# Where the operands of the second FFN products lie in memory, and a column of ones in place of a tile of ones

## The chip, the cores and the metric

The kernel runs on one NeuronCore of one Trainium2 chip. Its engines are TensorE (PE; its weight loads are listed apart as PEld), VectorE (DVE), ScalarE (ACT), GpSimd (POOL) and SyncE (SP, which issues DMAs). The metric is the device time of one execution in microseconds, as the median of several runs. The kernel before takes 958.76 us (3 runs, 957.85 to 961.19).

## The reference

One decoder layer in float32 on 512 tokens of width 1024: a half-step SwiGLU FFN, a token mixer, a second half-step FFN, each between two RMSNorms.

```
x = x + 0.5 * PostNorm_a(SwiGLU_1(PreNorm_a(x)))
x = x +       PostNorm_b(W_out [HGRN2_heads(h) ; mLSTM_heads(h)]),  h = PreNorm_b(x)
x = x + 0.5 * PostNorm_c(SwiGLU_2(PreNorm_c(x)))

def swiglu_ffn(x, w_in, w_out):
    gate, up = jnp.split(x @ w_in, 2, axis=-1)
    return (jax.nn.silu(gate) * up) @ w_out
```

The FFN's inner width is 2816. In this text "first products" are those of `x @ w_in`, "gated values" are `silu(gate) * up`, and "second products" those of the gated values with `w_out`. In the mixer's HGRN2 part the scores of neighbouring tokens (distance 1 within a pair) are sums over 128 features, which the kernel takes as a matmul with weights that are all one.

## The kernel before

**Three matmuls for one.** Every float32 operand of a large product is split in two parts of the type float32r: a rounded upper part (ACT, a copy) and the remainder (DVE, a subtraction). A product is upper x upper, upper x lower and lower x upper, all summed in PSUM. Many products of the FFNs also go through sums of blocks (a scheme with fewer block products), which is where names like p1 to p7, "quartered" and `common` come from.

**A matmul and its two operands.** Each matmul has weights, 128 x 128, which a separate load brings into the array, and a streamed operand of 256 or 512 columns. In the program each matmul loads its own weights. In the first products (L520) the FFN's weights `w` are the loaded side, and x (`xq`, or sums of its blocks in `sq`) is streamed. In the second products (L778 for plain ones, L786 for quartered ones) the gated values (`hs`, or `xq` where they are put there) are loaded and `w` is streamed. In the mixer L465 and L475 load `w` and stream `xq` with 256 columns; L136 to L138 load `xq` and stream `w` with 512.

**Where they lie.** An address here is that of a tile within a partition, in bytes mod 512, as the built program has it:

| operand | code | address mod 512 |
|---|---|---|
| `xq`, transposed x | tile's start | 160 |
| `w`, weights, four slots of 8192 bytes | `PAD + 2 * D * n` | 480 |
| `w` of 512 columns in the mixer, where a slot allows it | 16 elements earlier (`late`) | 416 |
| `hs`, gated values, both parts | `s_place`, `NEXT` = 16 elements | 288 |
| `hs` for sums of quarters, lower part | `apart`, `PAD` = 128 elements | 224 |
| gated values in an `xq` tile | `x_place`, `2 * NEXT` elements | 288 |
| sums of blocks of x in `sq` | `LATE` = 112 elements | 160 |
| one of them, its lower part | `part(0)` | 224 |

All steps inside an operand from one matmul to the next are multiples of 512 bytes.

**The order of the work.** `layer` runs the first FFN (`ffn_in`, then `ffn_out`), the mixer, and the second FFN. `ffn_in` goes through ORDER: for each of 11 pairs of column blocks it issues products of 24 matmuls (`prod`). `split` takes the next weights from their staging tile `raw` into a slot of `w` (ACT and DVE), `feed` keeps four slots filled, `drop` gives one back. `ffn_out` goes through two halves of the output columns. In each half it runs `plain` products (48 matmuls on L778) and `quartered` ones (42 on L786); `common` combines the block products on DVE (L754), and `add` puts the result into the accumulators. The last first-product (`p4` of the last pair, 24 matmuls on L520) is issued behind the first plain product of `ffn_out`. The last four plain products of the second half (LAST = 4) are done token block by token block in `chunk`, so that normalising a block can begin while the next is multiplied; transposes for the next stage (L295) lie between them. All engines run in the order that the program gives; nothing is chosen at run time.

**The tile of ones.** `masks` fills `ones`, 128 x 128, by a memset on POOL (L1043); `hgrn_level` uses it as weights once for each half of the heads (L1159), each in two passes. `one`, a column of 128 ones, is there already (L1028).

Of the kernel before, what the change touches and what calls it, by code (L numbers as in the profile page):

```python
# [8 lines left out]
F32 = mybir.dt.float32  # L9
# [12 lines left out]
EPS = 1e-6  # L22
RAW, WBUF, PAD, LATE, NEAR, NEXT = 3, 4, 128, 112, 48, 16
PAIRS = NF // 2
# [33 lines left out]


class Load:  # L60

# [16 lines left out]
class Layer:  # L78
    def __init__(self, ctx, tc, aps):
        self.tc, self.nc = tc, tc.nc  # L80
        self.__dict__.update(aps)
        nc = self.nc
        pool = lambda name, **kw: ctx.enter_context(tc.tile_pool(name=name, bufs=1, **kw))
        self.cp, self.wp, self.sp, self.psp = pool("cp"), pool("wp"), pool("sp"), pool("psp", space=PSUM)
        self.uid, self.hold = 0, ()
        self.wt, self.free, self.slot = None, deque(range(WBUF)), {}

        self.ident = self.cp.tile([P, P], F32, name="ident")
        make_identity(nc, self.ident)
        self.nhalf = self.cp.tile([P, 8], F32, name="nhalf")  # L90
        nc.gpsimd.memset(self.nhalf, -0.5)
        self.xs = self.cp.tile([P, NT, D], F32, name="xs")

        self.xq = [self.cp.tile([P, 2, KH, HALF], F32R, name=f"xq{n}") for n in range(4)]
        self.prm = self.cp.tile([P, 36], F32, name="prm")
# [96 lines left out]
    def load(self, ld):  # L192
        self.nc.sync.dma_start(self.raw[ld.key], ld.src)

    def split(self):

# [4 lines left out]
        if it.dst:  # L201
            w = it.dst()
        else:
            if self.wt is None:
                self.wt = self.wp.tile([P, 2 * D * WBUF + PAD], F32R, name="w")

            taken = {(n, late) for n, late, _ in self.slot.values()}
            fit = [(n, late) for late in (True, False) for n in self.free if (n - 1 if late else n + 1, not late) not in taken]
            n, late = next(f for f in fit if not f[1] or (it.key[0] == "mix" and b == 512))
            self.free.remove(n)  # L210
            o = PAD + 2 * D * n - 16 * late
            w = self.wt[:, o : o + 2 * D].rearrange("p (b k t) -> p b k t", b=2, k=a)
            self.slot[id(w)] = n, late, w
        hi, lo = self.both(w)
# [481 lines left out]

    def s_place(self, a=2, apart=False):

        t = self.hpool.tile([P, 2 * D + PAD], F32R, tag="s", bufs=3, name=self.nm("hs"))
        part = lambda o: t[:, o : o + D].rearrange("p (k t) -> p k t", k=a)  # L700
        return part(NEXT), part(D + (PAD if apart else NEXT))

    def x_place(self, *n):

        out = []
        for m in range(2):
            t = self.xq[n[m % len(n)]].rearrange("p b k t -> p (b k t)")
            o = 2 * NEXT + (D * m if len(n) == 1 else 0)
            out.append(t[:, o : min(o + D, 2 * D)])
# [25 lines left out]
    def h_sums(self, k2):  # L735
# [7 lines left out]
        for k in range(2):  # L743
            nc.vector.tensor_tensor(v[:, 2 * k + 1], a[:, k, 1], v[:, 2], op=ALU.subtract)
        hi, lo = self.s_place(4, True)
        self.two_parts(hi, lo, f.rearrange("p (k t) -> p k t", k=4))
# [284 lines left out]
    def masks(self, mc, mb):  # L1031
# [5 lines left out]
        for n, c in enumerate(LEVELS):  # L1037
# [4 lines left out]
            nc.gpsimd.affine_select(m, m, pattern=pat, compare_op=ALU.is_ge, fill=0.0, base=c - 1, channel_multiplier=-1)  # L1042
        self.ones = mb.tile([P, P], F32, name="ones")  # L1043
        nc.gpsimd.memset(self.ones, 1.0)
        self.eye = mb.tile([P, P], I32, name="eye")
# [86 lines left out]
    def hgrn_level(self, p, n, ke):  # L1132
# [25 lines left out]
        if c == 1:  # L1158
            nc.tensor.matmul(sc, self.ones, qe, start=True, stop=True)  # L1159
        else:  # L1160
# [501 lines left out]
```

## Time and profile before

| what | value |
|---|---|
| median of 3 runs | 958.76 us (957.85 to 961.19) |
| the profiled execution | 960.42 us |
| its span, first to last instruction | 958.7 us |
| mean granted TensorE clock | 0.997 of full speed |
| busy: TensorE, its weight loads, VectorE, ScalarE, GpSimd | 99%, 95%, 81%, 51%, 12% |
| instructions | 18146 |

One execution was profiled. A group of instructions is shown as line, engine, operation, output tile <- input tiles, shape, count, then the time in which at least one of them was busy, the mean duration of one in ns, and the idle time of the engine ahead of them with what ended it. Matmuls are pipelined, so their records overlap and a record is longer than the step from one matmul to the next. A view of windows gives for stretches of time the busy time and the count of records of each engine.

### The profile page before, as it was taken

The page shows a single profiled execution, that of the slowest core. Times are in us where ns is not written, and L with a number is a line of the kernel's source. Part 1 is how long each engine was busy: PE and PEld are TensorE (multiplying, and loading weights), DVE is VectorE, ACT ScalarE, POOL GpSimd, SP SyncE. Part 2 cuts the span into 40 slices and gives each one's busy share as a digit, 9 for nine tenths or more (in the row PEclk, how much of TensorE's full clock was granted, in tenths as well). Part 3 has the DMA queues.
Part 4 walks back from the last instruction along what each step waited for, and adds up shares of the span by engine and source line. Part 5 has one row for each costly group of instructions (what it writes and reads, how often), then busy time and mean ns, then how long its engine had stood idle before and what let it go on. Part 6 is the DMA issues. An engine that isn't in the chain of part 4 may idle for free.

```text
span 958.7 us, 18146 instructions
## 1 busy us (share of the span) xinstructions
PE 949.0 (99%) x7531; PEld 915.4 (95%) x7531; DVE 775.2 (81%) x1052; ACT 489.5 (51%) x691; POOL 119.1 (12%) x177
## 2 busy tenths in 40 slices
PE   9999999999999999999999999999999999999997
PEld 7999999999999999998887888899999999999997
DVE  6799989999788776688846565697998899977883
ACT  7645444455445456955622444664444444644541
POOL 2430000000001045200001210353000000000101
PEclk9999999999999999999999999999999999999999
DMA  9244343244232024421222124324334333224212
GB/s 320 77 134 130 116 128 111 89 133 131 87 96 84 23 78 123 111 66 44 70 64 67 45 80 139 112 67 133 111 110 121 111 110 101 66 89 133 73 39 88
DMA packets 81677, 96.13 MB, mean 100 GB/s; under 512 B 4117, under 2 KB 61497, under 8 KB 81594
## 3 DMA queue, kind: packets, MB, share of 16 engines
q1 hardware_dynamic: 81306, 94.44, 32.1%
q8 instruction: 59, 0.97, 0.4%
q10 hardware_dynamic: 288, 0.52, 0.2%
q14 instruction: 24, 0.20, 0.1%
HBM read 92.85 MB, written 2.10 MB: 99 GB/s over the span
## 4 chain that ended last, share of the span: by engine, by line
PE 62%; DVE 1%; ACT 0%; POOL 0%; issue 0%; POOLq 0%; DVEq 0%; ACTq 0%
PE ps L520 22%; PE ps L778 9%; PE ps L465 6%; PE ps L136 5%; PE ps L138 5%; PE ps L137 5%; PE ps L786 4%; PE ps L1163 2%; PE ps L475 1%; PE ps L295 1%; PE ps L1337 0%; PE ps L1248 0%; PE ps L1444 0%; PE ps L1417 0%; PE ps L1203 0%; PE ps L1441 0%
## 5 line engine op out<-in xcount | busy, mean ns | idle before, releaser
L220 ACT CAST w<-raw 128x1024 fp32r<-128x1024 f32 (+1 forms) x228 | 235.6, 1039 | 260.5 <-PE ps L520 94.5
L222 DVE TENSOR_TENSOR w<-raw,w 128x1024 fp32r<-128x1024 f32 (+1 forms) x228 | 281.9, 1243 | 46.9 <-ACT w L220 46.7
L520 PE MATMUL ps<-xq,w 128*128 128x256 f32 x2016 | 238.0, 277 | 0.0
L520 PEld LDWEIGHTS ps<-xq,w 128*128 128x128 f32 x2016 | 233.4, 188 | 0.0
L520 PE MATMUL ps<-sq,w 128*128 128x256 f32 x1440 | 171.0, 277 | 0.0
L520 PEld LDWEIGHTS ps<-sq,w 128*128 128x128 f32 x1440 | 167.4, 188 | 0.0
L778 PE MATMUL ps<-w,hs 128*128 128x256 f32 x1344 | 163.2, 281 | 0.0
L778 PEld LDWEIGHTS ps<-w,hs 128*128 128x128 f32 x1344 | 159.9, 189 | 0.3
L236 DVE TENSOR_TENSOR raw<-raw,raw 128x1024 f32<-128x1024 f32 x64 | 80.2, 1253 | 0.6
L136 PE MATMUL ps<-w,xq 128*128 128x512 f32 x192 | 79.0, 412 | 0.1
L138 PE MATMUL ps<-w,xq 128*128 128x512 f32 x192 | 75.0, 392 | 0.0
L137 PE MATMUL ps<-w,xq 128*128 128x512 f32 x192 | 74.9, 391 | 0.0
L383 POOL TENSOR_SCALAR col<-col 128x1 f32<-128x1 f32 x24 | 9.6, 401 | 500.9 <-ACT junk L382 500.8
L465 PE MATMUL ps<-xq,w 128*128 128x256 f32 x480 | 58.1, 283 | 0.0
L465 PEld LDWEIGHTS ps<-xq,w 128*128 128x128 f32 x480 | 56.9, 189 | 0.5 <-issue 0.5
L236 POOL TENSOR_TENSOR raw<-raw,raw 128x1024 f32<-128x1024 f32 x16 | 43.1, 2695 | 51.2 <-DVE w L222 42.0
L136 PEld LDWEIGHTS ps<-w,xq 128*128 128x128 f32 x192 | 36.1, 188 | 8.2 <-issue 0.8
L138 PEld LDWEIGHTS ps<-w,xq 128*128 128x128 f32 x192 | 36.1, 188 | 8.2 <-DVE xq L302 0.3
L137 PEld LDWEIGHTS ps<-w,xq 128*128 128x128 f32 x192 | 36.2, 189 | 6.7 <-issue 0.2
L713 ACT CAST hs<-hf 128x1024 fp32r<-128x1024 f32 x28 | 29.3, 1047 | 24.9 <-PE ps L786 24.9
L786 PE MATMUL ps<-w,hs 128*128 128x256 f32 x336 | 41.9, 282 | 0.0
L786 PEld LDWEIGHTS ps<-w,hs 128*128 128x128 f32 x336 | 40.6, 189 | 0.0
(251 smaller groups left out, 1151.8 us busy)
## 6 DMA issues: line engine op xcount, KB each, us to landing
raw<-in_ffn_w_in_dram SPq DMA_DIRECT2D x88, 512.0 KB, 3.8
raw<-in_ffn_w_out_dram SPq DMA_DIRECT2D x44, 512.0 KB, 4.0
raw<-in_w_mix_in_dram SPq DMA_DIRECT2D x28, 512.0 KB, 3.8
raw<-in_w_mix_out_dram SPq DMA_DIRECT2D x8, 512.0 KB, 3.9
out_dram<-xs SPq DMA_DIRECT2D x8, 256.0 KB, 2.1
xs<-in_x_dram SPq DMA_DIRECT2D x6, 256.0 KB, 6.8
gpost<-in_norm_post_dram SPq DMA_DIRECT2D x3, 512.0 KB
gpre<-in_norm_pre_dram SPq DMA_DIRECT2D x2, 512.0 KB, 4.1
```

What stands on the lines that cost most here:

```text
L136: mm(ps, sh, mh, start=start, stop=False, **kw)
L137: mm(ps, sh, ml, start=False, stop=False, **kw)
L138: mm(ps, sl, mh, start=False, stop=stop, **kw)
L220: nc.scalar.copy(hi, raw)
L222: nc.vector.tensor_tensor(lo, raw, hi.bitcast(F32), op=ALU.subtract)
L236: (nc.vector if late else nc.gpsimd).tensor_tensor(o, o, c, op=ALU.add)
L465: mm(ps[:, u0:u1], w[:, a, k, :], self.xop(k, b, u0, u1), start=k + n + m == 0, stop=k == ND - 1 and n == 2, skip_group_check=True,)
L520: self.nc.tensor.matmul(ps[:, c], wb[b][:, k, v], left[d][:, k, :], start=first and a + n + k == 0, stop=n == 2 and k == KH - 1, skip_grou ...
L713: self.nc.scalar.copy(hi, src)
L778: mm(out, a[kk][:, i * P : (i + 1) * P], w[:, b, kk, QUARTER * v : QUARTER * (v + 1)], start=begin and c == kk == n == 0, stop=kk == 1 and ...
L786: mm(ps[:, QUARTER * c : QUARTER * (c + 1)], A[a][:, c], B[b], start=begin and c == n == 0, stop=n == 2, skip_group_check=True,)
L1163: nc.tensor.matmul(sc[:, 64 * m : 64 * m + 64], k8[:, m], q8[:, m], start=True, stop=True)
```

## The change

The weights of the second products lie 80 elements (320 bytes) ahead of a slot's start or 48 elements behind it, which are both at 160 mod 512; the gated values lie at 480. `lie` looks for a place that no held weights overlap, in an order of preference for each kind: weights of the mixer with 512 columns still prefer 16 elements ahead of the slot (416), all others the slot itself (480). The tile `w` is one PAD (512 bytes) longer, and the order in which slots are handed out begins anew where none is held. The lower part of the gated values' sums loses its own place (`apart`). The tile `ones` is gone, and its 512 bytes; the matmul reads the column `one` 128 times with a step of zero.

```diff
-RAW, WBUF, PAD, LATE, NEAR, NEXT = 3, 4, 128, 112, 48, 16
+RAW, WBUF, PAD, LATE, NEAR, NEXT = 3, 4, 128, 112, 48, 64
...
+FREE = (1, 2, 3, 0)
+LIES = {"any": (0, -16, -80, 48), "mix": (-16, 0, -80, 48), "out": (-80, 48, 0, -16)}
...
-        self.wt, self.free, self.slot = None, deque(range(WBUF)), {}
+        self.wt, self.free, self.slot = None, deque(), {}
...
+    def lie(self, kind):
+
+        used = [o for _, o, _ in self.slot.values()]
+        at = LIES[kind]
+
+        first = 1 + (kind == "out")
+        tries = [(n, d) for n in self.free for d in (at[:first] if n < 2 else at[first - 1 :: -1])]
+        for n, d in tries + [(n, d) for d in at[first:] for n in self.free]:
+            o = PAD + 2 * D * n + d
+            if o + 2 * D <= self.wt.shape[1] and all(abs(o - a) >= 2 * D for a in used):
+                return n, o
...
-                self.wt = self.wp.tile([P, 2 * D * WBUF + PAD], F32R, name="w")
-
-            taken = {(n, late) for n, late, _ in self.slot.values()}
-            fit = [(n, late) for late in (True, False) for n in self.free if (n - 1 if late else n + 1, not late) not in taken]
-            n, late = next(f for f in fit if not f[1] or (it.key[0] == "mix" and b == 512))
+                self.wt = self.wp.tile([P, 2 * D * WBUF + 2 * PAD], F32R, name="w")
+            if not self.slot and it.key[0] != "mix":
+                self.free = deque(FREE)
+            n, o = self.lie("out" if it.key[1] == "out" else "mix" if it.key[0] == "mix" and b == 512 else "any")
             self.free.remove(n)
-            o = PAD + 2 * D * n - 16 * late
...
-    def s_place(self, a=2, apart=False):
+    def s_place(self, a=2):
 
         t = self.hpool.tile([P, 2 * D + PAD], F32R, tag="s", bufs=3, name=self.nm("hs"))
-        part = lambda o: t[:, o : o + D].rearrange("p (k t) -> p k t", k=a)
-        return part(NEXT), part(D + (PAD if apart else NEXT))
+        return [t[:, NEXT + D * m : NEXT + D * (m + 1)].rearrange("p (k t) -> p k t", k=a) for m in range(2)]
...
-            o = 2 * NEXT + (D * m if len(n) == 1 else 0)
+            o = PAD - LATE + NEXT + (D * m if len(n) == 1 else 0)
...
-        hi, lo = self.s_place(4, True)
+        hi, lo = self.s_place(4)
...
-        self.ones = mb.tile([P, P], F32, name="ones")
-        nc.gpsimd.memset(self.ones, 1.0)
...
-            nc.tensor.matmul(sc, self.ones, qe, start=True, stop=True)
+            nc.tensor.matmul(sc, self.one.broadcast_to([P, P]), qe, start=True, stop=True)
```

More of the change, by code (lines that the diff above doesn't have):

```diff
@@ L204, in split @@
             if self.wt is None:
-                self.wt = self.wp.tile([P, 2 * D * WBUF + PAD], F32R, name="w")
-            taken = {(n, late) for n, late, _ in self.slot.values()}
-            fit = [(n, late) for late in (True, False) for n in self.free if (n - 1 if late else n + 1, not late) not in taken]
-            n, late = next(f for f in fit if not f[1] or (it.key[0] == "mix" and b == 512))
+                self.wt = self.wp.tile([P, 2 * D * WBUF + 2 * PAD], F32R, name="w")
+            if not self.slot and it.key[0] != "mix":
+                self.free = deque(FREE)
+            n, o = self.lie("out" if it.key[1] == "out" else "mix" if it.key[0] == "mix" and b == 512 else "any")
             self.free.remove(n)
-            o = PAD + 2 * D * n - 16 * late
             w = self.wt[:, o : o + 2 * D].rearrange("p (b k t) -> p b k t", b=2, k=a)
-            self.slot[id(w)] = n, late, w
+            self.slot[id(w)] = n, o, w
         hi, lo = self.both(w)
```

## The prediction

> **What bounds the kernel.** I read the page's busy times first, then the chain, then the PE groups.
>
> ```profile
> span 958.7 us, 18146 instructions
> PE 949.0 (99%) x7531; PEld 915.4 (95%) x7531; DVE 775.2 (81%) x1052; ACT 489.5 (51%) x691; POOL 119.1 (12%) x177
> PE ps L520 22%; PE ps L778 9%; PE ps L465 6%; PE ps L136 5%; PE ps L138 5%; PE ps L137 5%; PE ps L786 4%; PE ps L1163 2%; PE ps L475 1%; PE ps L295 1%; PE ps L1337 0%; PE ps L1248 0%; PE ps L1444 0%; PE ps L1417 0%; PE ps L1203 0%; PE ps L1441 0%
> L520 PE MATMUL ps<-xq,w 128*128 128x256 f32 x2016 | 238.0, 277 | 0.0
> L778 PE MATMUL ps<-w,hs 128*128 128x256 f32 x1344 | 163.2, 281 | 0.0
> L786 PE MATMUL ps<-w,hs 128*128 128x256 f32 x336 | 41.9, 282 | 0.0
> ```
>
> TensorE is busy for 99% and nearly the whole chain is PE lines with no idle time before them. So the time is a count of matmuls times their pace, and nothing that is done beside them counts. The groups show the point of this case: the same form, 128x256, is recorded with 277 ns on L520 and 281 to 282 ns on L778 and L786.
>
> Records overlap, so the pace is read from windows in which PE is busy throughout: a window of length T holds (T + 0.28 us) / pace records, 0.28 us being the record of one.
>
> ```profile
> 106.00:121.90 15.90, 15.90 (x143) 15.90 (x142) 15.80 (x17) 7.46 (x10) 0.00 (x0) 1.00 0.45 133
> 144.00:160.00 16.00, 16.00 (x144) 16.00 (x143) 14.38 (x16) 7.55 (x10) 0.00 (x0) 1.00 0.31 99
> 163.00:179.00 16.00, 16.00 (x144) 16.00 (x143) 14.46 (x16) 7.54 (x10) 0.00 (x0) 1.00 0.32 101
> 187.00:198.00 11.00, 11.00 (x99) 11.00 (x98) 9.70 (x11) 5.89 (x8) 0.00 (x0) 1.00 0.31 97
> 209.00:221.00 12.00, 12.00 (x108) 12.00 (x107) 11.68 (x15) 8.96 (x13) 0.00 (x0) 1.00 0.48 133
> ...
> 234.00:314.00 80.00, 80.00 (x682) 80.00 (x681) 66.58 (x101) 39.46 (x56) 3.36 (x8) 1.00 0.31 95
> 834.00:930.00 96.00, 96.00 (x818) 96.00 (x817) 80.55 (x120) 47.29 (x64) 3.36 (x8) 1.00 0.26 83
> ```
>
> Columns: window, its length, then busy time and count of PE, PEld, DVE, ACT, POOL, the granted clock, the DMA. The five windows of the first products (L520) give 72.3 / 638 = 113.3 ns a matmul. Those of the second products (L778, L786) give 80.28 / 682 = 117.7 and 96.28 / 818 = 117.7 ns. The clock is 1.00 in all, and PEld is busy all the time: the weights of the next matmul are loaded while this one streams. DVE is busier in the short-paced windows (15.8 of 15.9 us) than in the long-paced ones (80.6 of 96), so the other engines aren't what lengthens them.
>
> **Why I take the addresses for the cause.** L778 itself goes at both paces, and so does L465 of the mixer:
>
> ```profile
> L778 PE MATMUL ps<-w,hs 128*128 128x256 f32 x427 | 51.4, 281 | 0.0
> ...
> L778 PE MATMUL ps<-w,hs 128*128 128x256 f32 x70 | 8.9, 276 | 0.0
> ...
> L465 PE MATMUL ps<-xq,w 128*128 128x256 f32 x32 | 3.8, 277 | 0.0
> ...
> L465 PE MATMUL ps<-xq,w 128*128 128x256 f32 x31 | 3.8, 281 | 0.0
> ...
> L520 PE MATMUL ps<-xq,w 128*128 128x256 f32 x63 | 7.7, 281 | 0.0
> ```
>
> These rows are groups in windows: L778 from 234 to 314 us (the products before the last four) and from 330 to 341 (the last four), L465 from 418 to 421.4 and from 424 to 427.4, L520 from 37 to 47. Code and addresses mod 512 bytes are the same in both rows of L778, and in both of L465. A stretch that starts short stays short, one that starts long stays long, and what precedes it decides. I call distance the start of what a matmul streams minus the start of the weights loaded beside it, mod 512 bytes. Inside L520, L465 and most of L778 it is 192. It changes at borders: when L520 hands over to L778, x at 160 streams beside gated values at 288, distance 384, and from L778 back to L520 it is 0. The view in order of time has such a border:
>
> ```profile
> 223.75 2.09 PE L520 MATMUL ps<-xq,w 128*128 128x256 f32 x17
> 225.68 5.82 PE L778 MATMUL ps<-w,hs 128*128 128x256 f32 x48
> 231.33 2.90 PE L520 MATMUL ps<-xq,w 128*128 128x256 f32 x24
> ```
>
> From a stretch's length, less one record, over its count less one: 1.81 / 16 = 113 ns, then 5.54 / 47 = 118 ns from the border on, then 2.62 / 23 = 114 ns after the next border. My reading: both paces hold themselves at distance 192; a jump of the distance or a stall throws the pair of streams into one or the other.
>
> **The change, part by part.** 1. Second products. The weights move from 480 to 160 mod 512, the gated values from 288 (and 224) to 480. The distance is 192 within L778 and L786, also where it was 256 (sums, lower part at 224), and now at the borders with L520 as well: both then stream from 160 beside weights at 480. The first products arrive at 113.7 ns (209 to 221 us: 12.28 / 108) and nothing jumps, so I expect the short pace to go on. How many matmuls have it to gain:
>
> ```profile
> 225.00:325.20 100.20, 63.47 (x528) 62.81 (x528) 1.00 0.28 86
> 830.00:930.20 100.20, 63.42 (x528) 62.79 (x528) 1.00 0.27 85
> ...
> 225.00:325.20 100.20, 35.77 (x294) 35.12 (x294) 1.00 0.28 86
> 830.00:930.20 100.20, 35.77 (x294) 35.12 (x294) 1.00 0.27 85
> ```
>
> The first two are L778 alone, the others L786 alone: 822 in each FFN, 1644 in all, times 117.7 - 113.3 = 4.4 ns: **7.2 us**. The last four products have little more to give; they run short already:
>
> ```profile
> 330.00:341.00 11.00, 11.00 (x100) 11.00 (x99) 5.68 (x10) 4.23 (x15) 3.92 (x10) 1.00 0.00 1
> ...
> 934.00:946.00 12.00, 12.00 (x108) 12.00 (x107) 5.10 (x10) 2.37 (x10) 2.77 (x7) 1.00 0.20 74
> ```
>
> That is 11.28 / 100 = 113 and 12.28 / 108 = 114 ns.
>
> 2. What is late next. Ahead of the last four products DVE adds the common parts into the accumulators:
>
> ```profile
> 324.45 2.48 DVE L754 TENSOR_TENSOR ps<-ps,hf 128x512 f32<-128x512 f32 x4
> ```
>
> That chain starts when the last quartered product is done, and PE has one plain product (48 matmuls) in the meantime. PE gains 48 x 4.4 = 0.2 us there and may wait that much longer; queued behind are the last four products. For two FFNs I give back **0.4 us** (bounds 0 and 0.4). DVE's 66.58 of 80 us become 66.6 of 77: no new bound.
>
> 3. Mixer weights of 512 columns. In the program 24 of their 192 groups of three matmuls go from 416 to 480 and 8 come back, 48 matmuls net. A window with groups at 480 and one with groups at 416:
>
> ```profile
> L138 PE MATMUL ps<-w,xq 128*128 128x512 f32 x7 | 2.8, 395 | 0.0
> ...
> L138 PE MATMUL ps<-w,xq 128*128 128x512 f32 x9 | 3.5, 390 | 0.0
> ```
>
> Windows from 437 to 443 and 574 to 580: at most 48 x 5 ns = 0.2 us, at least 0. I take 0, since the first window also holds stops between steps.
>
> 4. The column of ones. Four passes load weights by re-reading one element; no row has such a load. Nearest rows:
>
> ```profile
> L132 PEld LDWEIGHTS ps<-ident 128*128 128x128 f32 x14 | 3.3, 327 | 3.0 <-POOL ident masks.py:199 1.5 <-issue 1.5
> L1159 PEld LDWEIGHTS ps<-qe,ones 128*128 128x128 f32 x4 | 0.7, 188 | 0.1
> L1004 PEld LDWEIGHTS ps<-ident,rows 36*128 36x128 f32 x1 | 0.1, 134 | 0.1
> ```
>
> Four loads between 134 and 327 ns instead of 188: -0.2 to +0.6 us. It is nearest to its own row, so 0. The memset that goes is on POOL, 12% busy: 0, covered by PE.
>
> Order on every engine stays as it is, but for that memset, and all tiles behind it move by whole 512 bytes.
>
> Sum: 7.2 - 0.4 = 6.8 us. The profiled execution took 960.42 us (span 958.7 and 1.7 around it), so it would take 953.6. It lies 1.7 us above the median 958.76; against the median I forecast **952.0 us**.
>
> **The rivals.** A rule speaks against all this: the Trainium skill, page "SBUF — State Buffer", section "Who interferes with whom", gives TensorE one read port for the streamed operand and another for the weights, and says "PE and ACT never wait on anyone". By that rule the addresses give 0 and the time stays at 958.8. The trace leaves it open: L778's two paces at the same addresses fit the rule, the lengthening at the border at 225.68 us doesn't.
>
> *Addresses don't decide.* For it: L465 has 277 and 281 ns at the very addresses that the change chooses (160 and 480), and L520 has 281 from 37 to 47 us with them. If what is in the code of L778 and L786 (three of one accumulator, repeated weights) picks the long pace, it stays: 958.8. Against: L778 with the same code is short in the last four products. Chance 0.08.
>
> *Half of it.* One FFN is thrown into the long pace at its first border, by a wait there: 3.4 us instead of 6.8, so 955.4. For: a pace is taken over from what goes before. Against: both FFNs have the same order, and between 225 and 325 us PE is never idle. Chance 0.08.
>
> *Slower: a long run that nothing ends.* The jump to distance 0 that returned the 24 matmuls at 231.33 us to the short pace is gone. If the second products start long, these 24 and the last four products (192 in each FFN) are long too: 2 x 216 x 4.4 = 1.9 us more than now, 960.7. It decides only if L520 enters at the long pace, and the row from 209 to 221 us speaks against. Chance 0.06.
>
> **The numbers.** Forecast 0.78. Around it lie the unchanged stretches that go by chance: the mixer's L465 and L475, 576 matmuls that mostly run long now, would give up to 576 x 4.4 ns = 2.5 us if they fell short, and a spell at a lower clock after the first FFN comes or stays away:
>
> ```profile
> L465 PE MATMUL ps<-xq,w 128*128 128x256 f32 x480 | 58.1, 283 | 0.0
> L475 PE MATMUL ps<-xq,w 128*128 128x256 f32 x96 | 13.5, 302 | 1.6 <-DVE w L222 1.5
> ...
> 350.00:356.00 6.00, 4.47 (x26) 4.28 (x25) 5.61 (x8) 2.77 (x7) 2.29 (x3) 0.72 0.42 110
> ```
>
> A clock of 0.72 over 6 us is 1.7 us lost. So the forecast's own range is 949.3 to 955; up to 956 it takes in the half case, and leaves out the cases without a gain. A measurement of this kernel can't tell less than about 0.3% (2.9 us) from no change; below 955.9 is faster. Faster 0.84 (the forecast and most of the half case), same 0.12 (no effect, and most of the slower rival, which is +0.2%), slower 0.04.
>
> **What would show it.** Right: L778 (x1344) and L786 fall from 281 and 282 to 276 or 277 ns, the windows of the second products give 113 ns as L520 does, the groups of L520 and the loads keep theirs, and the 24 matmuls of L520 in between stay at 113. The add of L754 is followed by a PE wait longer by up to 0.2 us. Wrong: L778 still at 281, which makes the addresses innocent; L778 short but L786 long, which puts it on the repeated weights; a first FFN unlike the second, which makes it chance; or a gain under 5 us with both short, which means a wait that I don't see took it.

## The result, and the profile after

The changed kernel takes 950.99 us (median of 6 runs, 950.70 to 951.75) against 958.34 us of the kernel before in the same runs (957.24 to 961.19): a ratio of 0.9921 with a 95% interval of 0.9907 to 0.9935, so 6.2 to 8.9 us less. Its profiled execution took 950.96 us with a span of 949.2 us; the one before had 958.7.

The page of the changed kernel: span, busy times, and the groups that answer to those shown before. L537 is the old L520, L794 and L802 the old L778 and L786, L482 the old L465, L492 the old L475, L1173 the old L1159.

```profile
span 949.2 us, 18146 instructions
PE 938.8 (99%) x7531; PEld 905.0 (95%) x7531; DVE 774.5 (82%) x1052; ACT 489.4 (52%) x691; POOL 119.4 (13%) x176
...
L537 PE MATMUL ps<-xq,w 128*128 128x256 f32 x2016 | 237.9, 277 | 0.0
...
L794 PE MATMUL ps<-w,hs 128*128 128x256 f32 x1344 | 158.9, 277 | 0.6 <-DVE ps L770 0.6
...
L482 PE MATMUL ps<-xq,w 128*128 128x256 f32 x480 | 56.4, 278 | 0.0
...
L802 PE MATMUL ps<-w,hs 128*128 128x256 f32 x336 | 40.3, 276 | 0.0
```

TensorE is still busy for 99%, with the same 7531 matmuls. L794 and L802 have come down to the 277 and 276 ns of L537, which itself has not moved. Their busy time fell from 163.2 + 41.9 to 158.9 + 40.3 us: 5.9 us. New is an idle time of 0.6 us ahead of L794, waiting for L770 on DVE (the old L754).

The windows of the changed kernel; the columns are window, length, busy time and count of PE, PEld, DVE, ACT, POOL, clock, DMA:

```profile
228.00:320.00 92.00, 92.00 (x814) 92.00 (x814) 79.65 (x119) 47.44 (x64) 3.56 (x8) 1.00 0.27 87
...
822.00:918.00 96.00, 96.00 (x849) 96.00 (x849) 83.65 (x126) 50.16 (x69) 3.55 (x8) 1.00 0.27 89
```

Read as in the prediction: 92.28 / 814 and 96.28 / 849 are both 113.4 ns, where they were 117.7. And the border, in order of time:

```profile
222.82 2.66 PE L537 MATMUL ps<-xq,w 128*128 128x256 f32 x22
225.32 5.60 PE L794 MATMUL ps<-w,hs 128*128 128x256 f32 x48
230.76 2.88 PE L537 MATMUL ps<-xq,w 128*128 128x256 f32 x24
```

The 48 products behind the first border now go at 5.32 / 47 = 113 ns (118 before), and nothing happens at the next border.

### The profile page after: what moved, and what is told of

Read it like the earlier page. It is cut to its first block, busy times and chain, and to the rows that moved or that the text cites. A ratio compares the mean times of both kernels' runs of the same rounds, so it can differ in the third digit from the quotient of the medians.

```text
span 949.2 us, 18146 instructions
## 1 busy us (share of the span) xinstructions
PE 938.8 (99%) x7531; PEld 905.0 (95%) x7531; DVE 774.5 (82%) x1052; ACT 489.4 (52%) x691; POOL 119.4 (13%) x176
## 4 chain that ended last, share of the span: by engine, by line
PE 62%; DVE 1%; issue 0%; ACT 0%; POOL 0%; POOLq 0%; DVEq 0%; ACTq 0%
PE ps L537 23%; PE ps L794 8%; PE ps L482 6%; PE ps L143 5%; PE ps L145 5%; PE ps L144 5%; PE ps L802 3%; PE ps L1177 2%; PE ps L492 1%; PE ps L312 1%; PE ps L1351 0%; PE ps L1262 0%; PE ps L1458 0%; PE ps L1431 0%; PE ps L1217 0%; DVE w L239 0%
## 5 line engine op out<-in xcount | busy, mean ns | idle before, releaser
L237 ACT CAST w<-raw 128x1024 fp32r<-128x1024 f32 (+1 forms) x228 | 235.7, 1040 | 252.2 <-PE ps L537 92.0
L239 DVE TENSOR_TENSOR w<-raw,w 128x1024 fp32r<-128x1024 f32 (+1 forms) x228 | 281.8, 1242 | 42.0 <-ACT w L237 41.9
L537 PE MATMUL ps<-xq,w 128*128 128x256 f32 x2016 | 237.9, 277 | 0.0
L537 PEld LDWEIGHTS ps<-xq,w 128*128 128x128 f32 x2016 | 233.3, 188 | 0.0
L537 PE MATMUL ps<-sq,w 128*128 128x256 f32 x1440 | 171.0, 277 | 0.0
L537 PEld LDWEIGHTS ps<-sq,w 128*128 128x128 f32 x1440 | 167.4, 188 | 0.0
L794 PE MATMUL ps<-w,hs 128*128 128x256 f32 x1344 | 158.9, 277 | 0.6 <-DVE ps L770 0.6
L794 PEld LDWEIGHTS ps<-w,hs 128*128 128x128 f32 x1344 | 155.6, 188 | 0.9 <-issue 0.9
L143 PE MATMUL ps<-w,xq 128*128 128x512 f32 x192 | 78.9, 411 | 0.1
L145 PE MATMUL ps<-w,xq 128*128 128x512 f32 x192 | 74.9, 392 | 0.0
L144 PE MATMUL ps<-w,xq 128*128 128x512 f32 x192 | 74.9, 391 | 0.0
L482 PE MATMUL ps<-xq,w 128*128 128x256 f32 x480 | 56.4, 278 | 0.0
L482 PEld LDWEIGHTS ps<-xq,w 128*128 128x128 f32 x480 | 55.2, 188 | 0.5 <-issue 0.5
L802 PE MATMUL ps<-w,hs 128*128 128x256 f32 x336 | 40.3, 276 | 0.0
L802 PEld LDWEIGHTS ps<-w,hs 128*128 128x128 f32 x336 | 39.1, 188 | 0.0
```

The lines of the kernel that those rows point to most:

```text
L143: mm(ps, sh, mh, start=start, stop=False, **kw)
L144: mm(ps, sh, ml, start=False, stop=False, **kw)
L145: mm(ps, sl, mh, start=False, stop=stop, **kw)
L237: nc.scalar.copy(hi, raw)
L239: nc.vector.tensor_tensor(lo, raw, hi.bitcast(F32), op=ALU.subtract)
L482: mm(ps[:, u0:u1], w[:, a, k, :], self.xop(k, b, u0, u1), start=k + n + m == 0, stop=k == ND - 1 and n == 2, skip_group_check=True,)
```

## The experiments

In what follows "short" is the pace of 113.3 ns a matmul (records of 276 to 277 ns), "long" that of 117.7 ns (281 to 282 ns). A place is an address mod 512 bytes; "160 beside 480" streams from 160 while weights at 480 are loaded. The "pair" is what a matmul streams and the load that runs beside it, which is that of the next matmul: in the stretches of products looked at for this, in the traces of before, after and seven places, a load starts 1 to 5 ns after the start of the matmul ahead of its own.

| run | median us (runs) | ratio to the kernel before, 95% interval |
|---|---|---|
| column of ones alone | 957.67 (10) | 1.0004 [0.9994, 1.0014] |
| kernel before, all shifted by 192 bytes | 957.84 (10) | 1.0007 [0.9997, 1.0017] |
| changed kernel, all shifted by 320 bytes | 951.38 (4) | 0.9936 [0.9920, 0.9953] |
| changed kernel, one step aside | 951.31 (4) | 0.9934 [0.9919, 0.9949] |
| weights alone moved | 959.67 (10) | 1.0015 [1.0006, 1.0024] |
| gated values alone moved | 963.18 (4) | 1.0050 [1.0036, 1.0063] |
| changed kernel, eight steps aside | 953.62 (4) | 0.9953 [0.9940, 0.9967] |
| changed kernel, no 448 in the head | 951.29 (5) | 0.9925 [0.9912, 0.9939] |
| changed kernel, sixteen steps at 256 | 961.88 (4) | 1.0045 [1.0028, 1.0061] |
| kernel before, two steps aside | 951.83 (4) | 0.9932 [0.9916, 0.9949] |

Of two more one execution each was timed: seven places (1006.93 us) and short asides (1026.36 us).

### The column of ones alone

```diff
-        self.ones = mb.tile([P, P], F32, name="ones")
-        nc.gpsimd.memset(self.ones, 1.0)
...
-            nc.tensor.matmul(sc, self.ones, qe, start=True, stop=True)
+            nc.tensor.matmul(sc, self.one.broadcast_to([P, P]), qe, start=True, stop=True)
```

> The kernel before, with only the column of ones in place of the tile of ones; all operands of products stay where they were mod 512 bytes. Theory (two paces that hold themselves, 113.3 and 117.7 ns a matmul; a jump of the distance or a stall throws them from one into the other): 958.3 us, between 958.1 and 958.9, L778 and L786 stay at 281 to 282 ns a record. Rival (the column, or the code around it, brings part of the gain): below 956.

957.67 us beside 957.86 for the kernel before on the same chip: no difference. The loads of the ones in the changed kernel, with their shortest, median and longest duration in ns:

```profile
L1173 PEld LDWEIGHTS ps<-qe,one x4: 188/188/192, 397.0 to 449.3; 128*128 128x128 f32 x4
```

That is the 188 ns of the loads before. The groups of the page show something else as well:

```profile
span 955.4 us, 18146 instructions
...
L778 PE MATMUL ps<-w,hs 128*128 128x256 f32 x1344 | 163.2, 281 | 0.0
L465 PE MATMUL ps<-xq,w 128*128 128x256 f32 x480 | 56.4, 278 | 0.0
L786 PE MATMUL ps<-w,hs 128*128 128x256 f32 x336 | 41.9, 281 | 0.0
...
L475 PE MATMUL ps<-xq,w 128*128 128x256 f32 x96 | 12.2, 283 | 1.6 <-DVE w L222 1.5
```

L778 and L786 stand where they stood. But the mixer's L465 took 56.4 us here against 58.1 in the profile of before, and L475 12.2 against 13.5, with no operand of theirs moved. The prediction named a spell at a lower clock there, 0.72 from 350 to 356 us in the profile of before. Here the same window has none (window, length, PE, PEld, DVE, ACT, POOL, clock, DMA):

```profile
350.00:356.00 6.00, 4.48 (x40) 4.28 (x39) 5.62 (x8) 2.77 (x7) 2.44 (x3) 1.00 0.45 117
```

The two go together: of the fourteen profiles of this case three have such a spell (before, and the two shifted kernels of the next section, with 0.72 and 0.73), and in these three L465 took 58.0 or 58.1 us, in the other eleven 56.4 to 56.8. Nothing in the runs shows what brings the spell. The changed kernel's profile has none, and the same two low values (56.4 and 12.2), so of the 9.5 us between the two spans 3.0 are no effect of the change. The span of this run, 955.4 us, is the better one to compare with 949.2: 6.2 us.

### All places shifted

Unused bytes ahead of everything, 192 in the kernel before (as here) and 320 in the changed one (80 elements in place of 48):

```diff
+        self.cp.tile([P, 48], F32, name="ahead")
         self.ident = self.cp.tile([P, P], F32, name="ident")
```

> The kernel before with 192 unused bytes ahead of all tiles. Second products then stream weights from 160 beside gated values at 480, the very places of the changed kernel; first products stream x from 352 beside weights at 160. All distances, also those at the borders (384 in, 0 back), are as before. Theory (distances and what precedes decide, not places): 958.3 us, L778 and L786 at 281 to 282 ns. Rival (places mod 512 decide): L778 and L786 fall to 276 or 277 ns and the time to about 951, unless the first products get worse by it; L520 at 281 then.

> The changed kernel with 320 unused bytes ahead of all tiles. Second products then stream weights from 480 beside gated values at 288, the very places of the kernel before; no jump at the borders, all distances as in the changed kernel. Theory (distances): 951 us, L794 and L802 at 276 to 277 ns. Rival (places): back at 281 to 282 ns, 958 us.

The first stayed at 957.84 us, the second at 951.38. A window inside the second products, in the kernel before with its shift:

```profile
236.00:316.00 80.00, 80.00 (x682) 80.00 (x681) 65.83 (x101) 38.58 (x55) 3.36 (x8) 1.00 0.31 99
```

And in the changed kernel with its own:

```profile
230.00:310.00 80.00, 80.00 (x709) 80.00 (x708) 69.34 (x108) 42.01 (x58) 3.56 (x8) 1.00 0.30 93
```

80.28 / 682 = 117.7 ns at the very places that the change chose, and 80.28 / 709 = 113.2 ns at the places that it left. So no place is good or bad by itself. This falsifies the rival of the places, from both sides.

### The weights alone, the gated values alone

The changed kernel with the gated values back where they were, and the kernel before with `NEXT` = 64 and the gated values at 480, its weights not moved. Of the first, without the lines that give the lower part of the sums its own place again:

```diff
-RAW, WBUF, PAD, LATE, NEAR, NEXT = 3, 4, 128, 112, 48, 64
+RAW, WBUF, PAD, LATE, NEAR, NEXT = 3, 4, 128, 112, 48, 16
...
-            o = PAD - LATE + NEXT + (D * m if len(n) == 1 else 0)
+            o = 2 * NEXT + (D * m if len(n) == 1 else 0)
```

> The changed kernel with the gated values at 288 (and 224) as before: only the weights of the second products have moved, to 160. No border jumps in place of the stream; the distance inside the second products is 384, and 448 for the lower part of the sums. Single steps at 384 took 117 to 118 ns so far; no run shows a lasting one. Theory (the distance of 192 is what can be short): a lasting 384 is long, 117.7 ns and 958 us. Rival (each of the two moves brings its half): 954.6 us, 115.5 ns. Rival (the stream's place alone counts): 951 us.

> The kernel before with the gated values at 480: only they have moved, the streamed weights are at 480 too, so the distance inside the second products is 0, and the one from first to second products stays 192. The step at distance 0 took 117 ns so far; no run shows a lasting one. Theory (192 is what can be short): a lasting 0 is long, 117.7 ns a matmul or more, 958 us or above. Rival (each move brings its half): 954.6 us. Rival (the place of the loaded side alone counts): 951 us.

Either half of the change alone loses: 959.67 and 963.18 us. A window with the weights alone moved:

```profile
265.00:320.00 55.00, 55.00 (x466) 55.00 (x466) 46.55 (x70) 29.68 (x44) 3.36 (x8) 1.00 0.28 87
```

The same window with the gated values alone moved:

```profile
265.00:320.00 55.00, 55.00 (x461) 55.00 (x460) 45.95 (x70) 29.51 (x44) 3.36 (x8) 1.00 0.28 87
```

55.28 / 466 = 118.6 ns at a distance of 384 (mixed with some 448), and 55.28 / 461 = 119.9 ns at a distance of 0. The first is a mean: from start to start, the steps at 384 repeat in fives of some 118, 122, 120, 119 and 115 ns. In the second run that is (119.9 - 117.7) x 1644 = 3.6 us more than before, and up to 2.4 us (384 x 6.2 ns) in the last four products, which ran at some 113.7 ns before; 5.3 us were measured. The theory had put both at 117.7 or more; the distance does matter, and both moves are needed to keep 192.

### One step aside, eight steps aside

In the changed kernel, ahead of the first second product of each FFN, one matmul that loads from 288 (the first run), or eight that load from 288, of which seven stream from 480 (the second):

```diff
+                    if half == m == 0:
+                        mm(C[0][0][:, :QUARTER], h[0][:, 0, 80 : 80 + P], w[:, 0, 0, :QUARTER], start=True, stop=True, skip_group_check=True)
```

```diff
+                    if half == m == 0:
+                        for o in (80,) * 7 + (0,):
+                            mm(C[0][0][:, :QUARTER], h[0][:, 0, 80 : 80 + P], w[:, 0, 0, o : o + QUARTER], start=True, stop=True, skip_group_check=True)
```

> The changed kernel with one matmul more in each FFN, at the first border from first to second products: its weights are gated values at 288 mod 512, so that one step has the distance 384 and the next is back at 192. It writes a PSUM block that the next matmul into it starts anew, so the result is the same. Its own cost is 2 x 0.12 us. Theory (a jump throws the pair of streams, and a pace holds itself at 192): both FFNs run long from there to the last four products, the 24 matmuls of L537 in between too: 951.0 + 2 x (822 + 24) x 4.4 ns = 958.4 us; if only one FFN is thrown, 954.9. Rival (places or code decide for each matmul): 951.2 us, L794 and L802 at 276 to 277 ns.

> The changed kernel with eight matmuls more in each FFN at the first border: they load gated values at 288; seven stream from 480 and the eighth from 160. So the stream jumps from 160 to 480 one matmul behind the load, as at the border before, and comes back together with the load, at a distance of 192. They write a PSUM block that is started anew afterwards. Their own cost is 16 x 0.115 = 1.8 us over 951.2, 953.0. Theory (that border throws the pair into the long pace, and it holds at 192 also at the changed kernel's places): all 822 second products and 24 first products between them run long in both FFNs, 953.0 + 7.4 = 960.4; in one FFN, 956.7. Rival (the long pace belongs to streaming from 480 beside 288, not to what went before): 953.0 us, and only the eight are long.

Both expectations of the theory failed. One step aside: 951.31 us where 958.4 was expected. Eight steps: 953.62 where 960.4 was expected. The second run's view in order of time:

```profile
223.07 2.88 PE L537 MATMUL ps<-xq,w 128*128 128x256 f32 x24
225.79 1.10 PE L862 MATMUL ps<-w,hs 128*128 128x256 f32 x8
226.73 5.61 PE L794 MATMUL ps<-w,hs 128*128 128x256 f32 x48
```

The eight go at 0.82 / 7 = 117 ns, the 48 behind them at 5.33 / 47 = 113 ns. So steps like those of the old border do throw the pair into the long pace, but the way back to 160 beside 480 ended it. A jump need not throw the pair for good, and the step back must be counted as a second jump.

### No 448 in the head

Some of the products at the head of each FFN take weights that `ffn_in` keeps in `sq`, at distances of 448 and 256, and run long. Their weights were placed at 480, one part at 416:

```diff
-        self.stay = [self.place(t, KH) for t in sq]
-        self.stay[1] = (self.stay[1][:, 0], sq[1][:, D + NEAR : 2 * D + NEAR].rearrange("p (k t) -> p k t", k=KH))
+        at = lambda t, o: t[:, o : o + D].rearrange("p (k t) -> p k t", k=KH)
+        self.stay = [(at(t, NEAR if n == 1 else NEXT), at(t, D + NEXT)) for n, t in enumerate(sq)]
```

> The changed kernel with the weights that `ffn_in` keeps in `sq` (those of the first products c1, c3, c4 at the head of each FFN) placed at 480 and, for one part, 416, so that 226 of the head's matmuls have the distance 192 and 60 the distance 256, and none 448. In the changed kernel some 308 matmuls of the first head and 237 of the second run long. Theory (a stretch at 256 ends in the short pace at the next 192, as it does every 19 us in the first products): the heads turn short behind the first such stretch, up to 300 x 4.4 ns = 1.3 us and 237 x 4.4 ns = 1.0 us less, so 949 to 950 us. Rival (the head is long for another reason, such as waits for its first transfers): 951 us, the same windows at 281 ns.

951.29 us, no gain over the changed kernel: the expectation failed. Two groups of its trace, from 25.5 to 27.7 us and from 30.8 to 47 us; between them lie sixteen matmuls at distance 256:

```profile
L537 PE MATMUL ps<-xq,w 128*128 128x256 f32 x22 | 2.7, 276 | 0.0
...
L537 PE MATMUL ps<-xq,w 128*128 128x256 f32 x91 | 11.0, 281 | 0.0
```

The stretch at 256 did the opposite of what was expected: short ahead of it, long behind it, at the same places and the same distance of 192. That gave the next experiment its tool.

### Sixteen steps at 256

```diff
+                    if half == m == 0:
+                        for o in (112,) * 16:
+                            mm(C[0][0][:, :QUARTER], h[0][:, 0, o : o + P], w[:, 0, 0, :QUARTER], start=True, stop=True, skip_group_check=True)
```

> The changed kernel with sixteen matmuls more in each FFN at the first border: they stream from 160, as those around them, and load gated values at 416 (distance 256). They write a PSUM block that is started anew afterwards. Their own cost is 32 x 0.119 = 3.8 us over 951.2, 955.0. In the head of the run without 448, sixteen such steps at 27.7 us stood between a short stretch and a long one at the same places. Theory (the stretch at 256 moves the load against the stream until the pair is in the long pace, and that holds at 192): all 822 + 24 matmuls behind it run long in each FFN up to the last four products, 955.0 + 7.4 = 962.4. Rival (places relative to each other decide, so that 160 beside 480 is short again at once): 955.0 us.

961.88 us: the theory had 962.4, the rival 955.0. The windows of the second products, first and second FFN:

```profile
230.00:310.00 80.00, 80.00 (x682) 80.00 (x681) 65.18 (x102) 38.04 (x54) 3.37 (x8) 1.00 0.29 93
835.00:915.00 80.00, 80.00 (x682) 80.00 (x681) 65.12 (x103) 38.39 (x55) 3.37 (x8) 1.00 0.29 93
```

80.28 / 682 = 117.7 ns in both. The code of the second products, their addresses and distances are those of the changed kernel; only sixteen matmuls ahead of them differ, and the whole gain is gone, in 846 matmuls of each FFN. The long pace holds itself for 846 x 117.7 ns, some 100 us, at the places that the change chose.

### Seven places

At the first border of each FFN of the changed kernel, seven times sixteen matmuls at another place, and sixteen back at 160 beside 480 each time. `q` is the offset of the weights: in the first FFN it follows `o` one matmul later (so that load and stream jump together), in the second it has the value of `o`:

```diff
+                        self.aside += 1
+                        away = [o for o in (16, 32, 48, 64, 80, 96, 112) for o in (o,) * 16 + (0,) * 16]
+                        for j, o in enumerate(away):
+                            q = away[j - 1] if self.aside == 1 and j else o
+                            q = 0 if self.aside == 1 and not j else q
+                            mm(C[0][0][:, :QUARTER], h[0][:, 0, q : q + P], w[:, 0, 0, o : o + QUARTER], start=True, stop=True, skip_group_check=True)
```

> The changed kernel with 224 matmuls more in each FFN at the first border, seven times sixteen at another place (streams from 224, 288, 352, 416, 480, 32, 96, weights always 192 less) and each time sixteen back at 160 beside 480. In the first FFN stream and load move together, so that no step leaves the distance of 192; in the second the load moves one matmul ahead of the stream, as at the borders of the kernel before. They write a PSUM block that is started anew afterwards; 448 x 0.116 = 52 us, so 1003 us. Theory (a jump of the distance throws the pair, a pace holds at 192): no change of pace at all in the first FFN, changes in the second, which last until the next jump. Rival (the pace belongs to the place, measured from where the pair last settled: 160 is short, some other places are long): the same places are long in both FFNs, and each return to 160 is short.

The pace of each sixteen, read from groups in windows inside them, in the order of time ("back" is 160 beside 480):

| FFN | 224 | back | 288 | back | 352 | back | 416 | back | 480 | back | 32 | back | 96 | back |
|---|---|---|---|---|---|---|---|---|---|---|---|---|---|---|
| first, together | long | short | long | long | short | long | long | long | short | long | short | long | long | short |
| second, load ahead | long | short | long | long | short | long | long | long | short | long | long | long | short | long |

Four of the rows, from the first FFN: at 224 (225.6 to 227.2 us), back (227.9 to 229.0), and back from 480 (242.3 to 243.9) and from 96 (249.7 to 251.3):

```profile
L867 PE MATMUL ps<-w,hs 128*128 128x256 f32 x16 | 2.0, 281 | 0.0
...
L867 PE MATMUL ps<-w,hs 128*128 128x256 f32 x12 | 1.5, 276 | 0.0
...
L867 PE MATMUL ps<-w,hs 128*128 128x256 f32 x16 | 2.0, 281 | 0.0
...
L867 PE MATMUL ps<-w,hs 128*128 128x256 f32 x17 | 2.1, 276 | 0.0
```

Both expectations fall. The theory had no change of pace in the first FFN, where no step leaves the distance of 192: there were ten. The rival had the return to 160 always short: it is short three times in fourteen. Its other half, the same pace at the same place in both FFNs, holds at five of the seven places and fails at 32 and 96. What remains is plainer. Within five steps each sixteen goes at one of the two paces. From the short pace every one of the ten jumps led to the long one; from the long pace nine of eighteen led to the short one. The last jump left the first FFN short and the second long, and there they stayed, for the same products at the same places (windows from 252 and from 877 us):

```profile
252.00:346.00 94.00, 94.00 (x832) 94.00 (x831) 75.44 (x110) 47.44 (x64) 3.55 (x8) 1.00 0.25 85
877.00:972.00 95.00, 95.00 (x809) 95.00 (x808) 73.21 (x107) 47.29 (x64) 3.36 (x8) 1.00 0.26 84
```

94.28 / 832 = 113.3 ns and 95.28 / 809 = 117.8 ns, in one execution of one program.

### Short asides

Six series in each FFN: sixteen steps at 256 to make the pace long, sixteen at 160 beside 480, then 1, 2, 3, 4, 6 or 8 steps aside with the loads kept, and sixteen at 160 beside 480.

```diff
+                        away = [(0, 112)] * 16 + [(0, 0)] * 15
+                        for z in (1, 2, 3, 4, 6, 8):
+                            for o, q in away + [(16 * self.aside, 0)] * z + [(0, 0)] * 16:
+                                mm(C[0][0][:, :QUARTER], h[0][:, 0, q : q + P], w[:, 0, 0, o : o + QUARTER], start=True, stop=True, skip_group_check=True)
```

> The changed kernel with 306 matmuls more in each FFN at the first border, in six series: sixteen that load from 416 (distance 256, which threw the pair into the long pace in both FFNs before), sixteen at 160 beside 480, then 1, 2, 3, 4, 6 or 8 that stream from 224 (first FFN) or 288 (second FFN) while the loads stay at 480, and sixteen at 160 beside 480 again. They write a PSUM block that is started anew afterwards; 612 x 0.117 = 72 us, so 1023 us. Theory (a pace holds itself at a constant place until a jump): the sixteen behind the steps at 416 are long each time; the eight at 224 in the first FFN end in the short pace, as the same eight do at 218 us in every run, and the 844 products behind run short. Open, and asked here: how few steps aside are enough, and whether 288 does it too. Rival (the same place always has the same pace): all sixteens at 160 beside 480 are short.

All twelve sixteens behind the steps at 256 are long. Behind the steps aside:

| steps aside | 1 | 2 | 3 | 4 | 6 | 8 |
|---|---|---|---|---|---|---|
| stream from 224 | long | short | long | short | short | short |
| stream from 288 | long | long | short | long | short | long |

Around the two steps at 224, from 233.3 to 234.9 us and from 235.7 to 236.9 us:

```profile
L866 PE MATMUL ps<-w,hs 128*128 128x256 f32 x16 | 2.0, 281 | 0.0
...
L866 PE MATMUL ps<-w,hs 128*128 128x256 f32 x13 | 1.6, 276 | 0.0
```

At 224 two matmuls are enough to end a long stretch and three are not; at 288 it is the other way round. So neither the place nor the number of steps decides alone, and what does is not shown.

### Two steps aside in the kernel before

If both paces hold at any place, the kernel before needs no moved weights: two steps aside, once in each FFN, should do. All operands of the second products at the places before (the lower part of the sums at 288 as well), the column of ones, and:

```diff
             v = self.pull()
+            if begin and half == 0:
+                for _ in range(2):
+                    mm(M["p7"][:, :QUARTER], S(0)[0][:, 0], self.flat(v[:, 0])[:, 16 : 16 + QUARTER], start=True, stop=True, skip_group_check=True)
             product(M["p7"], S(0), quarter(v, 0), begin)
```

> The kernel before, with all operands of the second products at the places before (480 streamed, 288 loaded; the lower part of the sums at 288 too, so that the distance is 192 throughout), the column of ones, and two matmuls more in each FFN inside the first quartered product: they stream from 32 while the loads stay at 288, and write a PSUM block that is started anew afterwards. In the run of short asides, two such steps (64 bytes further, loads kept) ended a long stretch. Theory (both paces hold at any place, and two steps aside end the long one): the 709 second products behind them in each FFN run short, 957.7 - 2 x 709 x 4.4 ns + 4 x 0.12 = 952.0 us, and the second products ahead of them stay long. Rival (the changed kernel's places are needed for the short pace): 958.2 us, L778 at 281 ns throughout. If one FFN alone is thrown: 955.1.

951.83 us: 952.0 was expected by the theory, 958.2 by the rival. In order of time, in the first FFN (L803 are the two steps):

```profile
239.53 1.58 PE L786 MATMUL ps<-w,xq 128*128 128x256 f32 x12
...
241.65 0.40 PE L803 MATMUL ps<-w,hs 128*128 128x256 f32 x2
241.89 2.22 PE L786 MATMUL ps<-w,hs 128*128 128x256 f32 x18
```

And the windows behind them, in the first and the second FFN:

```profile
242.50:318.00 75.50, 75.50 (x669) 75.50 (x668) 65.08 (x99) 41.12 (x56) 3.56 (x8) 1.00 0.29 92
842.00:918.00 76.00, 76.00 (x673) 76.00 (x672) 65.59 (x99) 41.40 (x56) 3.55 (x8) 1.00 0.28 91
```

1.30 / 11 = 118 ns ahead of the two steps, 1.94 / 17 = 114 ns behind them, and then 75.78 / 669 and 76.28 / 673, both 113.3 ns, over 76 us. The lower part of the sums at 288 was not tried without the two steps, so its share is not measured apart. The order in time speaks for the steps: ahead of them eighteen quartered matmuls at a constant distance of 192 are long, behind them they are short.

## Why the prediction was right

**The bound and its reading.** TensorE stayed the bound at 99%; the gain is matmuls of a shorter step, as the two paces in the windows had said.

**Second products: 7.2 us.** The windows give 113.4 ns where 113.3 was forecast; 1644 x (117.7 - 113.4) = 7.1 us. Added up in the traces from the start of each matmul to the start of the next, the paces are 117.85 and 113.33 ns, so 7.4 us. Right in size, and in its cause as far as the runs reach: what goes on at a border is taken over by all that follows. The shifted kernels show that the address as such is innocent, the sixteen steps at 256 that the same addresses go long when something ahead of them disturbs the pair, and the two steps aside that the old addresses go short.

**Its mechanism was half right.** The prediction read both paces as holding themselves at distance 192, thrown by "a jump of the distance or a stall". That they hold is shown. But the throw is not tied to the distance: with load and stream jumping together, the distance never left 192 and the pace changed ten times. In the seven places every move out of the short pace did it, and a return is a move as well. The change worked since it leaves no move at all from 219 us to the last four products: x and weights stream from 160 and all loads come from 480. The steps at distance 256 (lower part of the sums) and those at 384 and 0 at the borders were the moves of before. In the profile of before the long pace starts at the border, at 225.68 us, ahead of the first quartered product; no run has the steps at 256 without the borders, so what they alone would do there stays open.

**What is late next: 0.4 us given back, bounds 0 and 0.4.** The wait was there, and above the bound: 0.6 us of idle time by the page. It cost more than that. A record is longer than a step, and idle time counts from the record's end; from start to start, the step with the wait takes 0.58 us where a short one takes 0.11, so 0.47 us in each FFN and 0.9 in both. The wait also had a consequence that the sum didn't hold. The changed kernel at the second FFN's last four products, first its view in order of time, then a window (length, PE, PEld, clock, DMA):

```profile
920.20 4.83 PE L794 MATMUL ps<-w,hs 128*128 128x256 f32 x39 [0.30 <-DVE ps L770]
```

```profile
921.00:942.00 21.00, 21.00 (x181) 21.00 (x180) 1.00 0.20 74
```

These go at 21.28 / 181 = 117.6 ns; before it was 114. Over 192 matmuls that is 0.7 us lost. The same wait can be followed by the short pace: so it is in the first FFN of this execution (15.28 / 134 = 114 ns from 322.5 to 337.5 us), and in the second FFN of the run with one step aside:

```profile
920.52 4.68 PE L794 MATMUL ps<-w,hs 128*128 128x256 f32 x39 [0.30 <-DVE ps L770]
```

```profile
921.00:942.00 21.00, 21.00 (x187) 21.00 (x187) 1.00 0.21 76
```

21.28 / 187 = 113.8 ns. What decides which pace comes out of a stall is not shown.

**The parts together.** Added up from start to start, with the waits, the 822 second products of each FFN took 96.87 us before and 93.62 after, so 6.5 us less in the two FFNs (7.4 - 0.9). The last four products took 0.5 us more in both together. That is 6.0 us less by these lines, beside 6.2 us between the span of the changed kernel and that of the column alone. The 5.9 us of the two groups in the section on the result is no test of this sum: these groups hold neither the waits nor the 348 second products whose gated values lie in an `xq` tile.

**The mixer's 512 columns and the column of ones: 0.** Right: the three groups of 512 columns took 78.9, 74.9 and 74.9 us after, and 79.0, 74.9 and 75.0 before; the loads kept their 188 ns, and the column alone gave 1.0004.

**The time.** 952.0 forecast, 950.99 measured, inside the range of 949.3 to 955. That it is so close is in part luck. The sum had 6.8 us, the traces account for 6.0 to 6.2, and the medians lie 7.35 us apart, with 6.2 as the lower end of the interval; the 1 us between is not accounted for by the change. The parts that the prediction left to chance are of this size: between the two profiles the mixer's L465, named with up to 2.5 us, gave 1.7 us and L475 1.3 us, and both come with the spell at the lower clock, which the prediction named beside them as a thing apart. The run of the column alone shows that this isn't the change's doing.

**The rivals.** "Addresses don't decide" in its strong form, by which the time stays, fell with the result. The rule named with it, from the Trainium skill, page "SBUF — State Buffer", section "Who interferes with whom", gives the streamed operand and the weight load ports of their own, on which TensorE waits for no one. The runs differ from it: moving the streamed operand alone took the mean step to 118.6 ns and moving the loaded one alone to 119.9, while a shift of all tiles together left it at 117.7 or 113.2. So the pace depends on where the two lie to each other, and the measurement decides. What makes it depend is not shown. "Half of it" didn't occur in the changed kernel, though its mechanism exists: one FFN short and the other long is what the seven places left behind. The slower rival, "a long run that nothing ends", didn't occur either, but the sixteen steps at 256 produced it: 846 long matmuls in each FFN, and 961.88 us with 3.8 us of that for the added matmuls.

**What stays open.** The runs don't say what differs in the pair between the two paces, nor why even and odd numbers of steps aside differ at 224 while the outcome at 288 follows no such order. The start of the load shows no difference: it lies 3.3 ns in the mean behind the start of the matmul ahead in both FFNs of the seven places, of which one is short and the other long; the load itself is recorded with 187.7 ns in the short one and 189.1 in the long. It wasn't tried, either, to end the long stretches at the head of each FFN (300 and 237 matmuls, at most 537 x 4.4 ns = 2.4 us) with two steps aside behind the last transposes. Moving the weights while the tile of ones stays wasn't tried, as its 512 bytes make the room for them.

## What to carry to other kernels

Where one line of matmuls has two mean durations in different stretches (here 276 and 281 ns), look at what changes at the start of each stretch, not at the stretch: the operands' places mod 512 bytes of what is streamed and of what is loaded beside it. Keep both unchanged across as many matmuls as possible, over borders between stages too, and move both or neither: half of this change alone cost 0.2% and 0.5%. Before moving tiles, try two matmuls with a moved stream at the start of the long stretch; here they brought the kernel before, with the lower part of its sums moved as well, from 957.94 to 951.83 us, which is the whole gain of the change within its uncertainty.

## What the runs showed of the hardware that was not expected

- A stream of matmuls with 256 columns of float32r at full clock has at least two paces that hold for more than 90 us at the same addresses, 113.3 and 117.7 ns; in one execution the same products of the two FFNs went at one each.
- At a lasting distance of 0 the step is 119.9 ns, at one of 384 (with some 448) 118.6 ns in the mean; no short stretch was seen at either.
- A shift of all tiles by 192 or 320 bytes changed nothing (1.0007, and 0.9936 beside 0.9921).
- With the stream 64 bytes aside, one step and back left a long stretch long, two made it short, three didn't; with it 128 bytes aside, two didn't and three did.
- A spell at a lower clock near 350 us (0.72 or 0.73 over a window of 6 us) came in three of fourteen profiles, and the mixer's L465 behind it took 58.0 to 58.1 us instead of 56.4 to 56.8.
